# Neighbourhood attention on one core: two heads' scores in the two row halves of the array, operands loaded one pair ahead

## The chip, the core and the metric

The kernel runs on one core of a Trainium2 chip. The core has TensorE (PE, with its weight loads listed apart as PEld), VectorE (DVE), ScalarE (ACT), GpSimd (POOL) and SyncE (SP, which here only issues DMAs); each takes its own instructions in order and waits on semaphores for the others. The metric is the device time of one execution in microseconds (us); lower is better.

## The reference

A diffusion backbone of two layers works on 2048 latent tokens (a grid of 32 rows and 64 columns) of width 1024 and on 256 context tokens. The first ("even") layer has dense attention and a gated linear scan. The second ("odd") layer, which the change is about, is neighbourhood attention with 16 heads of 64: each token looks at a window of 8 x 16 grid neighbours, with a learned bias, and at all 256 context tokens, and one softmax goes over both.

```python
s_lat = jnp.einsum('bqhd,brkhd->bhqrk', qr, kb, preferred_element_type=jnp.float32) * scale
s_lat = s_lat + bias.astype(jnp.float32)[None]
s_lat = jnp.where(col_mask[None, None, :, None, :], s_lat, -jnp.inf).reshape(bsz, h, GRID_W, kr * GRID_W)
s_ctx = jnp.einsum('bqhd,bchd->bhqc', qr, k_ctx, preferred_element_type=jnp.float32) * scale
p = jax.nn.softmax(jnp.concatenate([s_lat, s_ctx], axis=-1), axis=-1).astype(v.dtype)
o = jnp.einsum('bhqk,bkhd->bqhd', p[..., :kr * GRID_W], vb.reshape(bsz, kr * GRID_W, h, d))
return o + jnp.einsum('bhqc,bchd->bqhd', p[..., kr * GRID_W:], v_ctx)
...
y = jnp.dot(o.reshape(h.shape[0], h.shape[1], C_WIDTH) * jax.nn.silu(z_x), w_out)
```

## The kernel before

The stages run one after the other, each with its own pools of tiles: the even layer up to about 1885 us, the odd layer's queries and keys (`odd_qk`) to about 2540, its values and gates (`odd_vz`) to 2970, the attention (`odd_attention`) to about 3368, and the output projection, woven with its end, to 3532. Products that need more than one pass are split in a high and a low part, so that a score is q·k = kh·qh + kl·qh + kh·ql.

`odd_vz` weaves two streams: gemms for values and gates (lines 131 to 133), and, for every head and query, a maximum of its scores (matmuls 1696 and 1703, DVE 1709 with the bias table `mtab`). To that table POOL adds a row mask and a column mask (lines 1681 and 1682). The maxima M go to memory with a minus sign, and later enter the scores as one more row, so that the exponentials cannot overflow.

`odd_attention` works on eight pairs of heads, j = 0 to 7. A pair has 20 steps in a fixed order: c0, c1, l0 to l3, c2, l4 to l7, c3, l8 to l15. Context step c*n* takes the 512 queries of block *n* against the 256 context keys (two key tiles, u = 0 and 1); local step l*n* takes the 128 keys of tile *n* against the rectangle of queries that can see them (264 to 480 wide in PE's scores).

- **Scores** (lines 1792 to 1794): for each head and key tile two matmuls into a bank `st` of 512 (four banks in turn): K's high and low halves stacked on 128 rows against the high part of Q, which stands there twice; and 65 rows, K's high part and a row of ones against Q's low part and the row M.
- **Bias and exponential**: in a local step DVE adds the bias table to each head's bank (line 1954, in 1 to 4 rectangles a head), into a tile `opt` (11 buffers) that both heads share; ACT (line 108, the helper `act`) takes the exponential. A context step has no bias, and ACT reads the bank directly, 512 at a time.
- **Tails**: a step's P·V is put off on a list `pend`. When six steps stand there, four are issued (`flush(4)`): matmuls on column halves of the array, one head in each, lines 1805 (context) and 1827 (local), into tiles `o`. The sums of P for the denominators are kept in `oacc`, by POOL (1815 and 1833) and DVE (1817).
- **Denominators**: two flushes after a block of 512 queries is complete, `finish_block` (lines 1001 to 1008) sums `oacc` over the keys on PE, again in column halves, and divides: ACT takes Ln and Exp of the sums, and DVE has three operations. POOL stores the result.
- **Loads** (line 113, all on SP in program order): keys of the local steps come in chunks of 512 (`kt`), one chunk ahead; queries, tables and values of the next pair during the pair. POOL adds the mask to both heads' tables (line 1790).

The order on each engine is the order of the program, but for places where an instruction is put behind another by hand (`issue_after`). Tiles come in turn out of their buffers, and an instruction waits until the last readers of that buffer are done.

## Time and profile before

| | us |
|---|---|
| three executions | 3533.73, 3535.8, 3543.46 |
| median | 3535.8 |
| span of the profiled execution (its own time is not listed apart) | 3532.0 |
| PE busy | 3447.5 (98%) |
| DVE busy | 2431.0 (69%) |
| ACT busy | 1450.9 (41%) |
| POOL busy | 1246.5 (35%) |

The span is the stretch between the first and the last instruction of one execution; the three times contain a little more than that. PE's ends are modelled, so it is safer to read the start of one matmul to the start of the next than the length of one. A row of a group or of the timeline reads: line, engine, operation, output tile <- input tiles, shape; "64*128" is a row half of the array (64 rows), "128*64" a column half; "x4" is four such instructions in a row. What stands behind "<-" in brackets is the instruction or the DMA that ended the idle time.

Four groups of the attention that tell what its parts cost (count, total us, mean ns, idle time before them):

```profile
L1805 PE MATMUL o<-opt,ov 128*64 128x512 f32 x256 | 62.8, 606 | 0.0
L1954 DVE TENSOR_TENSOR opt<-st,tab 128x248 f32<-128x248 f32 x64 | 25.9, 405 | 23.7 <-ACT rl L108 23.7
L108 ACT ACTIVATE opt<-st 128x512 f32<-128x512 f32 x128 | 68.6, 603 | 33.9 <-PE st L1794 32.8 <-ACT opt L108 0.9
L1833 POOL TENSOR_TENSOR oacc<-oacc,opt 128x744 f32<-128x744 f32 x32 | 52.8, 1649 | 0.6
```

### The profile page before, as it was taken

What the parts mean: (1) busy time and instruction counts of PE and PEld (TensorE: products, weight loads), DVE (VectorE), ACT (ScalarE), POOL (GpSimd) and SP (SyncE); (2) the same over time, 40 slices, a digit from 0 to 9 for tenths busy, and PEclk for the clock granted to TensorE, in tenths of its full rate; (3) what the DMA queues carried; (4) which work ended last, traced back from release to release, by engine and by line L of the source; (5) the groups of instructions that cost most, each with busy time, mean ns of one, the idle gap of its engine ahead of it and who ended that gap; (6) DMA issues with size and microseconds to landing.
All of it is one profiled execution on the core that took longest, in us unless ns stands there. A gap on an engine that the chain in (4) does not pass through costs nothing.

```text
span 3532.0 us, 54046 instructions
## 1 busy us (share of the span) xinstructions
PE 3447.5 (98%) x19460; PEld 2667.4 (76%) x19460; DVE 2431.0 (69%) x4798; ACT 1450.9 (41%) x2647; POOL 1246.5 (35%) x1400
## 2 busy tenths in 40 slices
PE   8999999999999999999999999999999999999999
PEld 6888987888896666665557878888788887555577
DVE  4677756888886777768876655444478884666775
ACT  4545552111113454546664345445322223555532
POOL 1343431111111333422211134334344443888842
PEclk9999999999999999999999999999999999999999
DMA  7555555233325242334525665455844547888684
GB/s 255 149 157 159 150 143 152 94 110 92 90 78 169 63 134 81 104 109 138 174 87 140 129 191 144 137 157 144 259 153 161 166 141 208 224 214 210 195 235 75
DMA packets 379838, 527.28 MB, mean 149 GB/s; under 512 B 34746, under 2 KB 254346, under 8 KB 373124
## 3 DMA queue, kind: packets, MB, share of 16 engines
q1 hardware_dynamic: 326692, 405.85, 39.8%
q0 software_dynamic: 29856, 82.14, 9.3%
q10 hardware_dynamic: 23024, 35.85, 2.9%
q8 instruction: 154, 2.52, 0.3%
q14 instruction: 112, 0.92, 0.1%
HBM read 344.92 MB, written 196.60 MB: 153 GB/s over the span
## 4 chain that ended last, share of the span: by engine, by line
PE 82%; DMA 6%; DVE 5%; ACT 2%; POOL 2%; issue 2%; SPq 0%; DVEq 0%; ACTq 0%; POOLq 0%
PE st L1175 10%; PE gm L133 10%; PE gm L131 10%; PE gm L132 10%; PE av L1085 7%; PE mx L705 4%; PE st L1793 2%; PE o L1827 2%; PE pu L1364 2%; PE o L1364 2%; PE st L1794 2%; PE pj L1364 1%; PE o L1805 1%; PE st L1364 1%; PE mx L1703 1%
## 5 line engine op out<-in xcount | busy, mean ns | idle before, releaser
L706 DVE TENSOR_REDUCE mm<-mx 128x1 f32<-128x512 f32 (+1 forms) x656 | 389.1, 627 | 83.6 <-PE mx L705 76.6
L108 ACT ACTIVATE apt<-st 128x1024 f32<-128x1024 f32 (+1 forms) x296 | 300.2, 1015 | 304.7 <-PE st L1175 285.5
L1182 DVE TENSOR_TENSOR acc<-acc,apt 128x1024 f32<-128x1024 f32 x256 | 341.0, 1332 | 83.0 <-ACT apt L108 64.2
L1175 PE MATMUL st<-aq,akh 64*128 64x512 f32 x1728 | 312.1, 408 | 1.2 <-ACT apt L108 0.9
L1085 PE MATMUL av<-apt,av 128*64 128x512 f32 x1152 | 267.5, 602 | 0.0
L1954 DVE TENSOR_TENSOR opt<-st,tab 128x64 f32<-128x64 f32 (+10 forms) x576 | 144.6, 315 | 146.9 <-PE st L1794 101.3
L705 PE MATMUL mx<-mk,mq 96*128 96x512 f32 (+1 forms) x656 | 236.0, 373 | 4.2 <-DMA mq<-QC 3.6
L1833 POOL TENSOR_TENSOR oacc<-oacc,opt 128x576 f32<-128x576 f32 (+5 forms) x192 | 223.5, 1186 | 40.5 <-ACT rl L108 15.0
L1175 PE MATMUL st<-aq,akl 64*128 64x512 f32 (+1 forms) x1152 | 230.6, 390 | 0.0
L108 ACT ACTIVATE u<-gm 128x352 f32<-128x352 f32 (+1 forms) x140 | 68.6, 497 | 373.7 <-PE gm L133 205.9
L1175 PEld LDWEIGHTS st<-aq,akh 64*128 64x128 f32 x1728 | 152.8, 185 | 82.8 <-ACT apt L108 29.1
L1709 DVE CUSTOM_DVE_ANT_1 mx<-mx,mtab 128x217 f32<-128x217 f32 (+14 forms) x576 | 182.2, 340 | 34.7 <-PE mx L1703 25.7
L1085 PEld LDWEIGHTS av<-apt,av 128*64 128x64 f32 x1152 | 76.7, 137 | 136.5 <-issue 135.5
L108 ACT ACTIVATE opt<-opt 128x930 f32<-128x930 f32 (+8 forms) x130 | 104.5, 805 | 105.9 <-DVE opt L1954 102.3
L705 PEld LDWEIGHTS mx<-mk,mq 96*128 96x128 f32 x656 | 121.7, 189 | 16.5 <-issue 4.0
L1175 PEld LDWEIGHTS st<-aq,akl 64*128 64x128 f32 (+1 forms) x1152 | 112.2, 184 | 22.9
L1698 DVE TENSOR_REDUCE mm<-mx 128x2 f32<-128x512 f32 x128 | 88.3, 690 | 43.1 <-PE mx L1696 41.7
L220 POOL TENSOR_TENSOR oss<-oss,mhalf 128x8 f32<-128x8 f32 x68 | 113.4, 1667 | 5.0
L131 PE MATMUL gm<-w1h,hhi 128*128 128x512 f32 x280 | 111.6, 399 | 0.0
L133 PE MATMUL gm<-w1h,hlo 128*128 128x512 f32 x280 | 110.3, 394 | 0.0
L1793 PE MATMUL st<-q,kt 128*128 128x480 f32 (+5 forms) x256 | 99.3, 390 | 11.0 <-DVE opt L1954 6.4
L132 PE MATMUL gm<-w1l,hhi 128*128 128x512 f32 x280 | 109.6, 392 | 0.0
(699 smaller groups left out, 9747.3 us busy)
## 6 DMA issues: line engine op xcount, KB each, us to landing
q<-Q SPq DMA_DIRECT2D x48, 512.0 KB
H<-x ACTq DMA_DIRECT2D x32, 512.0 KB
adaw<-ada_w SPq DMA_DIRECT2D x64, 256.0 KB
wraw<-w_od SPq DMA_DIRECT2D x64, 256.0 KB
K1t<-okt POOLq DMA_DIRECT2D x32, 512.0 KB, 9.7
kt<-K1t SPq DMA_DIRECT2D x32, 512.0 KB
x<-H SPq DMA_DIRECT2D x31, 512.0 KB
mtab<-rpb_q SPq DMA_DIRECT2D x16, 899.0 KB
```

Of the source, the lines that this page charges most:

```text
L108: return self.nc.scalar.activation(out, in_, func, **kw)
L131: self.nc.tensor.matmul(out, lh(k), rh(k), start=start and j == 0, stop=False)
L132: self.nc.tensor.matmul(out, lh(k), rl(k), start=False, stop=False)
L133: yield self.nc.tensor.matmul(out, ll(k), rh(k), start=False, stop=stop and j == n - 1)
L705: mm = nc.tensor.matmul(ps[:, :w], q[:A_QK, (t % 6) * P : (t % 6) * P + P], k[:A_QK, k0 : k0 + w], start=True, stop=True)
L706: nc.vector.tensor_reduce(out=m[:, t, n : n + 1], in_=ps[:, :w], axis=AX.X, op=ALU.max)
L1085: mm = nc.tensor.matmul(O[j, nb][i * 64 : i * 64 + 64, :w], V[j, kt // TT][:, kt % TT, i * 64 : i * 64 + 64], pts[:, i, :w], start=n == 0, ...
L1175: mm = nc.tensor.matmul(ps[:, o // 64, :w], k[o : o + r, kb, kq], Q[o : o + r, qb, :w], start=m == 0, stop=m == 4)
L1182: added = nc.vector.tensor_tensor(out=acc[:, :, :w], in0=a[:, :, :w], in1=pts[:, :, :w], op=ALU.add)
L1364: self.mm = self.nc.tensor.matmul(ps, x[:, k, :], y, start=start and k == 0 and n == 0, stop=k == self.H4 - 1 and n == 2, skip_group_check ...
L1709: nc.vector.tensor_tensor_reduce(out=s, in0=s, in1=tb[:, ri : ri + rn, ci : ci + cn], scale=1.0, scalar=-3e38, op0=ALU.add, op1=ALU.max, a ...
L1833: self.psum = nc.gpsimd.tensor_tensor(out=a, in0=a, in1=pts[:, :, a0 - r0 : a1 - r0, :], op=ALU.add)
```

## The change

**Scores.** Each head gets a row half of the array (64 rows). A score has four terms, kh·qh, kl·qh, kh·ql and ones·M, and for each term the two heads' matmuls stand next to each other. M is a tile of zeros in which only rows 0 and 64 hold the two heads' maxima, against a tile of ones. Both heads of a step (in a context step, of one key tile) write one tile `st` of two banks, of which there are two in place of four single banks. One DVE addition adds the bias for both heads; one exponential takes 1024 in a context step.

**Denominators.** `finish_blocks` treats two blocks at once: the sums of blocks 0 and 1, and those of 2 and 3, take one of the two `st` tiles; ACT copies them out, and takes Ln and Exp of 1024. `pend` holds five steps and gives two at a time (`flush(2)`).

**Loads.** Queries and keys of a pair are tiles of both heads (high and low part, without copies), in two sets of pools `oaA` and `oaB`, and the next pair's are loaded at steps 3 to 6. The stored keys `K1t` have another layout, so that `odd_qk` stores them with two DMAs instead of four. The pools stand on the left side of the memory.

**Masks.** The tables come with -1e30 filled in where a key is out of the window, so POOL adds no masks, in `odd_vz` and in the attention, and `maskq` and `maskk` are not loaded.

```diff
-            bank = lambda: self.tl(pp, [P, 512], "st", bufs=4)
+            both = lambda: self.tl(pp, [P, 2, 512], "st", bufs=2)
...
-            def scores(ps, k1, k2, q1, q2):
-                nc.tensor.matmul(ps, k1, q1, start=True, stop=False)
-                return nc.tensor.matmul(ps, k2, q2, start=False, stop=True)
+            def scores(ps, ks, qs, j):
+                terms = [(K[j][0], Q[j][0]), (K[j][1], Q[j][0]), (K[j][0], Q[j][1]), (None, M[j % 2])]
+                for n, (k, q) in enumerate(terms):
+                    for i in range(2):
+                        s = slice(i * 64, i * 64 + 64)
+                        mm = nc.tensor.matmul(ps(i), ones[s] if k is None else k[s, ks], qs(q[s]), start=n == 0, stop=n == 3)
+                return mm
...
+            def finish_blocks(bbs, j, O, acc):
+                n = len(bbs)
+                den = both()
+                for b, bb in enumerate(bbs):
+                    for i, a in enumerate(sums(acc, bb)):
+                        mm = nc.tensor.matmul(den[i * 64 : i * 64 + 64, b, :], self.mtwos[:], a, start=True, stop=True)
+                dc, rc, ln = exps(), exps(), self.tl(lp, [P, 2, 512], "rl", bufs=1)
+                self.act(dc[:, :n], den[:, :n])
+                self.act(ln[:, :n], dc[:, :n], AF.Ln, scale=-1.0)
+                self.act(rc[:, :n], ln[:, :n], AF.Exp, scale=-1.0)
+                nc.vector.tensor_tensor(out=ln[:, :n], in0=dc[:, :n], in1=rc[:, :n], op=ALU.mult)
+                for b, bb in enumerate(bbs):
+                    o = O.pop(bb)[:].rearrange("p r c -> p (r c)")
+                    nc.vector.scalar_tensor_tensor(out=o, in0=ln[:, b], scalar=2.0, in1=o, op0=ALU.add, op1=ALU.mult)
+                    nc.vector.tensor_tensor(out=rc[:, b], in0=o, in1=rc[:, b], op=ALU.mult)
...
-                                bias = nc.vector.tensor_tensor(out=pt[:, d[0], d[1]], in0=ps[:, d[0], d[1]],
-                                                               in1=tabs[j][i][:, ri : ri + rn, ci : ci + cn], op=ALU.add)
+                                bias = nc.vector.tensor_tensor(out=pt[:, :, ro : ro + rn, co : co + cn],
+                                                               in0=ps[:, :, ro : ro + rn, d + co : d + co + cn],
+                                                               in1=tabs[j][:, :, ri : ri + rn, ci : ci + cn], op=ALU.add)
...
-                    if len(pend) == 6:
+                    if len(pend) == 5:
                         with self.tc.issue_after(mm.ins):
-                            flush(4)
+                            mm = flush(2)
```

The first place is on PE, in pair 3 around the first denominators that pair 2 leaves behind (`mtwos` is a tile of constants). Before, the order there is: the end of context step c1 (`kc`), the tails of four local steps, one block's denominators, then local scores:

```order
L1793 MATMUL st_30008<-q_5211_29706,kc_5235_29807 128x512
L1794 MATMUL st_30008<-q_5212_29707,kc_4848_28046 128x512
L1827 MATMUL o_29748<-opt_29877,ov_29238 64x3x24 x2
L1827 MATMUL o_29845<-opt_29877,ov_29238 64x8x24 x2
...
L1001 MATMUL st_30032<-oacc_5179_29576,mtwos_63 64x512 x2
L1793 MATMUL st_30047<-q_5185_29595,kt_5246_29874 128x288
L1794 MATMUL st_30047<-q_5186_29596,kt_4850_28048 128x288
L1793 MATMUL st_30054<-q_5211_29706,kt_5246_29874 128x288
L1794 MATMUL st_30054<-q_5212_29707,kt_4850_28048 128x288
```

In the changed kernel the tails of two local steps and the denominators of two blocks follow context step c0, and both key tiles of c1 and local step l0 come behind them (`om` is the tile of maxima):

```order
L1787 MATMUL st_30357<-om_4850_27978,ones_27976 128x512 x2
L1817 MATMUL o_30143<-opt_30259,ov_29567 64x3x24 x2
L1817 MATMUL o_30240<-opt_30259,ov_29567 64x8x24 x2
L1817 MATMUL o_30143<-opt_30290,ov_29567 64x3x31 x2
L1817 MATMUL o_30240<-opt_30290,ov_29567 64x8x31 x2
L1838 MATMUL st_30378<-oacc_5135_29953,mtwos_63 64x512 x4
L1787 MATMUL st_30395<-qh_29965,kh_29984 128x512 x2
...
L1787 MATMUL st_30406<-qh_29965,kh_29984 128x512 x2
...
L1787 MATMUL st_30417<-qh_29965,kh_29984 128x288 x2
```

The run of column halves moved one step up and is shorter by two tails; three score tiles in a row (30395, 30406, 30417) now share two buffers with the denominators' tile (30378).

The second place is ACT around the same denominators. Before, the exponentials of both context steps are done when Ln (`rl`) and Exp (`rc`) of one block come, and local exponentials follow:

```order
L108 ACTIVATE opt_29995<-st_30004 128x512
L108 ACTIVATE opt_29995<-st_30008 128x512
L108 ACTIVATE rl_30035<-st_30032 128x512
L108 ACTIVATE rc_30036<-rl_30035 128x512
L108 ACTIVATE opt_30046<-opt_30046 128x2x288
```

After it, with the copy of the denominators, Ln and Exp of 1024 ahead of the two exponentials of c1:

```order
L108 ACTIVATE opt_30355<-st_30346 128x1024
L108 ACTIVATE opt_30366<-st_30357 128x1024
L108 ACTIVATE opt_30383<-st_30378 128x1024
L108 ACTIVATE rl_30385<-opt_30383 128x1024
L108 ACTIVATE opt_30384<-rl_30385 128x1024
L108 ACTIVATE opt_30404<-st_30395 128x1024
L108 ACTIVATE opt_30415<-st_30406 128x1024
L108 ACTIVATE opt_30418<-opt_30418 128x2x288
```

The exponential of c1's first tile (30395) moved behind three operations on the denominators.

The third place is the first loads of the attention on SP, before:

```order
L113 DMA q_4852_28054<-Q 64x2048 x2
L113 DMA q_4853_28055<-Q 64x2048
L113 DMA q_4853_28055<-M 1x2048
L113 DMA kt_4854_28060<-K1t 128x2x512
L113 DMA kt_4850_28048<-K1t 64x2x512
L113 DMA ov_28063<-V 128x16x128
L113 DMA tab_4856_28065<-rpb_k 128x1034
L113 DMA tab_4857_28066<-rpb_k 128x1034
L113 DMA ov_28069<-maskk 128x1034
L113 DMA kc_4859_28073<-K1t 128x2x256
L113 DMA kc_4848_28046<-K1t 64x2x256
L113 DMA q_4860_28076<-Q 64x2048 x2
```

and after:

```order
L113 DMA kh_27982<-K1t 128x256
L113 DMA kl_27983<-K1t 128x256
L113 DMA qh_27980<-Q 128x1024
L113 DMA ql_27981<-Q 128x1024
L113 DMA om_4848_27974<-M 1x2048 x2
L113 DMA kh_27982<-K1t 128x512
L113 DMA kl_27983<-K1t 128x512
L113 DMA tab_27992<-rpb_k 128x2x1034
L113 DMA qh_27980<-Q 128x1024
L113 DMA ql_27981<-Q 128x1024
L113 DMA ov_27996<-V1c 128x2x128
L113 DMA ov_27996<-V 128x16x128
```

The context keys and the first half of both query parts moved to the front; the values' load moved from the seventh place to behind all queries.

305 lines of the change are left out of this document (132 added, 173 removed).

## The prediction

> **What bounds the kernel now.** I read the page's busy shares first (TensorE is busy for 98% of the span), then a table of windows over the stages that the change touches, because an average over the program says nothing about one stage. In each row: the window, its length, then busy time of PE, PEld, DVE, ACT and POOL, the granted clock, the DMA share and GB/s.
>
> ```profile
> 2540.00:2945.00 405.00, 402.60 (x1994) 338.72 (x1995) 316.85 (x1353) 105.17 (x177) 177.45 (x149) 1.00 0.50 159
> 2972.94:2986.60 13.66, 13.40 (x38) 9.62 (x38) 5.68 (x26) 6.68 (x11) 2.55 (x2) 0.50 0.96 274
> 3108.02:3153.48 45.46, 44.29 (x306) 27.22 (x305) 29.54 (x89) 25.36 (x41) 38.89 (x35) 1.00 0.87 222
> ```
>
> The first row is the stage of the gemms and row maxima, where the masks go from POOL: PE has 402.60 of 405 us, so less work on POOL is worth nothing there. The third is one head pair of the attention (from its first context score to the next pair's): 45.46 us, of which PE fills 44.29, POOL 38.89, DVE 29.54, ACT 25.36. So PE sets the pair, and only what it executes, or waits for inside a pair, counts. The second row is the start of the attention: 13.66 us at half clock, so 6.8 us lost. Why it starts cold is in PE's timeline (start, length, instruction, idle time before it):
>
> ```profile
> 2969.51 0.39 PE L133 MATMUL gm<-w1h,hlo 128*128 128x512 f32 x1
> 2972.62 1.33 PE L1793 MATMUL st<-q,kc 128*128 128x512 f32 x3 [2.72 <-DMA q<-Q]
> ```
>
> PE idles 2.72 us for the first queries. Over the whole attention, PE's list of waits (total, times, longest) names two more kinds:
>
> ```profile
> PE st L1793 <- DVE opt L1954: 6.8, 19, 1.7
> PE st L1794 <- DMA kt<-K1t: 1.7, 4, 0.7
> PE st L1793 <- DMA kt<-K1t: 1.6, 2, 1.1
> ```
>
> **1. The scores themselves: 0.** A step had four full matmuls (two heads, two terms); it gets eight in row halves, which are four slots if both halves run at once. Full slots, and row-half pairs of the even layer's attention (each x2 is a pair, the x4 two):
>
> ```profile
> 3109.68 0.39 PE L1793 MATMUL st<-q,kc 128*128 128x512 f32 x1
> 3109.91 0.40 PE L1794 MATMUL st<-q,kc 65*128 65x512 f32 x1
> 1304.57 0.40 PE L1175 MATMUL st<-aq,akh 64*128 64x512 f32 x2
> 1304.81 0.39 PE L1175 MATMUL st<-aq,akl 33*128 33x512 f32 x2
> 1305.04 0.62 PE L1175 MATMUL st<-aq,akh 64*128 64x512 f32 x4
> ```
>
> Start to start is 0.23 us for one full matmul and 0.24 and 0.23 for a pair. Same slots, same widths: nothing won or lost. P·V and denominators keep their matmuls too.
>
> **2. Switches between scores and column halves: +0.6 us a pair.**
>
> ```profile
> 3111.84 0.39 PE L1794 MATMUL st<-q,kc 65*128 65x512 f32 x1
> 3112.16 2.28 PE L1827 MATMUL o<-opt,ov 128*64 128x72 f32 x32
> 3244.59 1.02 PE L1001 MATMUL st<-oacc,mtwos 128*64 128x512 f32 x4
> 3245.54 0.43 PE L1793 MATMUL st<-q,kt 128*128 128x352 f32 x1
> 3245.81 0.33 PE L1794 MATMUL st<-q,kt 65*128 65x352 f32 x1
> ```
>
> The last score to P·V takes 0.32 us in place of 0.23; two denominator slots take 0.95 in place of the 0.86 that P·V slots of that width have; and the first score behind takes 0.27 for a slot of some 0.17 (352 wide). So 0.2 us a round trip. PE's order holds 7 column runs in a pair now and 10 after (two tails at a time instead of four): +0.6 us.
>
> The Trainium skill, TensorEngine Tiling (Array Packing), Key Properties, says that changing the tiling mode, and not just the tile, drains TensorE: a rule against this change, and the trace agrees, with 0.09 us at each of these seams. It gives no price, so the sum goes by the rows.
>
> **3. PE's waits inside a pair: +0.5 us.** Widths at the slot rates above give 38.4 us of array work a pair, before and after. 45.46 less 38.4 less 7 × 0.2 leaves 5.7 us of waits now (where a matmul starts late, the list above counts only what its modelled predecessor leaves idle). Those go with the four banks that were handed round singly; in their place come two double tiles. I walked the new order on PE, ACT and DVE for one pair with these durations (group rows: count, busy, mean ns; timeline rows of ACT):
>
> ```profile
> L1954 DVE TENSOR_TENSOR opt<-st,tab 128x465 f32<-128x465 f32 x64 | 38.1, 634 | 30.4 <-POOL oacc L1833 19.8 <-PE st L1794 10.7
> L1954 DVE TENSOR_TENSOR opt<-st,tab 128x240 f32<-128x240 f32 x64 | 25.5, 398 | 4.7 <-PE st L1794 4.6
> 1299.21 1.02 ACT L108 ACTIVATE apt<-st 128x1024 f32<-128x1024 f32 x1
> 1300.14 0.59 ACT L108 ACTIVATE gqT<-gl 128x512 f32<-128x512 f32 x1
> ```
>
> A double ACT operation lasts 1.02 us and blocks ACT for 0.93. A double bias addition is not in the trace: the two DVE rows give (634 − 398)/225 = 1.05 ns an element over some 146 ns, so 930 elements are about 1.12 us (bounds: 0.63, one of now, and 2 × 0.634 = 1.27). The worst place is the denominator run ahead of context chunk 1. On ACT stand, in order, the copy of the denominators, Ln, Exp, and only then the exponentials of the two new score tiles. From the end of the run: copy done at 0.25 + 1.02 = 1.3, the exponential behind Ln and Exp starts at 0.25 + 3 × 0.93 = 3.0 and ends at 4.1. PE does c1u0 (four slots, 0.93), waits 0.3 for the copy's tile, does c1u1, and stands at 7 × 0.33 = 2.3 before l0, which needs the tile of c1u0: **a wait of about 1.9 us**. Behind it queue all later matmuls. The second denominator run costs 0.7 the same way, double bias additions with two tiles cost 0.2 to 0.5 at five more places (1.7), and at each of the ten returns to scores some 0.15 is left of the release of a tile that the column run did not cover (1.5). Sum: 1.9 + 0.3 + 0.7 + 1.7 + 1.5 = 6.1, say 6.2 us. Bounds: 3.5 us, if tiles come free as early as the four banks do, and 8.5, if DVE's five operations of the denominators also stand ahead of a bias addition each time.
>
> So a pair costs +1.1 us; pairs 1 to 7 have the denominators in them: **+8**.
>
> **4. The clock after that wait: +4.** Half clock comes in steps of 3.41 us, after windows like these:
>
> ```profile
> 3321.10:3324.52 3.42, 1.67 (x8) 0.68 (x6) 3.42 (x6) 2.60 (x5) 2.37 (x2) 1.00 0.72 222
> 3324.52:3327.93 3.41, 3.41 (x9) 2.96 (x10) 3.41 (x9) 2.34 (x5) 3.41 (x4) 0.50 0.73 183
> 3426.92:3430.33 3.41, 1.75 (x8) 1.44 (x9) 3.41 (x5) 0.63 (x1) 1.62 (x2) 1.00 0.56 156
> 3430.33:3433.74 3.41, 1.25 (x6) 0.71 (x5) 0.53 (x1) 0.60 (x1) 2.77 (x2) 1.00 1.11 198
> ```
>
> With PE busy 1.67 us of 3.42 the next window is at 0.50; with 1.75 of 3.41 it stays at 1.00. So about 1.7 us of idle time in one window is the point. Mine of 1.9, with 0.3 ahead, is just over it, and fits whole in a window about half the time: 7 × 1/2 × 1.7 us = 6 if it is as long as walked, 0 if it is 0.3 shorter; I take 4.
>
> The Trainium skill, TensorE: Matmul & The Clock Gate, Part 1, says the clock halves after an idle window of some 3.4 us, so a wait of 1.9 us would do nothing; by it the sum would be 4 us lower. The trace disagrees: half a window of idle time was enough at 3321.
>
> **5. The start: −9.5.** Loads on SP now, the last matmul of the gemm that the first new load waits for, and POOL's memsets and a store of values:
>
> ```profile
> 2936.65 1.73 SPq L113 DMA_DIRECT2D q<-Q  x3
> 2951.22 9.73 SPq L113 DMA_DIRECT2D kc<-K1t  x2
> 2961.01 1.92 SPq L113 DMA_DIRECT2D q<-Q  x3
> 2946.66 0.39 PE L133 MATMUL gm<-w3h,hlo 128*128 128x512 f32 x1
> 2945.72 1.84 POOL L1759 MEMSET kt<- 1x1024 f32 x2
> 2962.99 0.57 POOL L1614 DMA_DIRECT2D V1c<-ovz  x1 [8.46 <-ACT ovz L108]
> ```
>
> Six whole query parts (twice the high one) of 512 KB, tables, a mask and values precede what the first score needs. After, the first score needs the context keys (0.25 MB) and half of the queries (1 MB), first in SP's order; they wait for the gemm with w3 (2946.66), and at the 274 GB/s of the window at 2972.94 1.25 MB take 5 us. So they land near 2955, ahead of the gemms' end at 2969.7: 2.7 us of waiting and 6.8 of half clock go. POOL clears a row tile of 2048 first, which by the row (two of 1024 in 1.84) ends near 2950. What is late next: the first values, whose load stands behind the store of 2962.99, with the other key chunks and pair 1's loads queued behind it on SP; the first P·V needs them some 7 us after 2970, so they still have 12 us. Bounds: 0 (rival c) and 9.5.
>
> **6. Key chunks: −5.** They were loaded just ahead; a pair ahead, the waits of 1.7 + 1.6 us go, and with them one half-clock window behind two of them (−1.7):
>
> ```profile
> 3239.00:3242.40 3.40, 3.40 (x23) 2.85 (x25) 2.19 (x12) 1.28 (x2) 3.40 (x3) 0.53 0.50 157
> ```
>
> High parts are no longer loaded twice, so the DMA share of 0.87 falls as well.
>
> **7. POOL's masks, half the DVE instructions, two stores for four of keys: 0.** PE covers them (402.60 of 405). Within a pair, the masks are two additions of 2.4 us on POOL:
>
> ```profile
> L1790 POOL TENSOR_TENSOR tab<-tab,maskk 128x1034 f32<-128x1034 f32 x14 | 33.3, 2398 | 0.0
> ```
>
> POOL falls from 38.9 to about 34 us of 46, DVE from 29.5 to 25, ACT grows by the two copies (+1.9): none is the bound over a pair. The output projection gets other buffers but the same order: 0, ±4.
>
> **Sum.** +8 + 4 − 9.5 − 5 = −2.5. The profiled span is 3532.0 and the runs are 3533.73, 3535.8 and 3543.46, so it stands for an execution at the lower end, about 1.7 us longer than its span; the difference is applied to the median: 3535.8 − 2.5 = 3533.
>
> **Rivals.** (a) *The waits are hidden.* Two double tiles let PE run ahead as well as four banks did, and the wait behind the denominators stays under the clock's point: part 3 takes its lower bound, 3.5 us in place of 6.2, and part 4 nothing. 7 × −2.7 − 4 = −23: 3510. For it speaks that the even layer's attention, with the same double tiles and 1.02 us exponentials, hardly waits for them; against it, that no Ln and Exp stand between its scores:
>
> ```profile
> L1175 PE MATMUL st<-aq,akh 64*128 64x512 f32 x1728 | 312.1, 408 | 1.2 <-ACT apt L108 0.9
> ```
>
> (b) *Slower: every denominator run drops the clock for two windows.* Place: l0 of pairs 1 to 7; price: 6.8 us at half clock, 3.4 each, 24 in place of 4; it decides from 1.7 us of idle time in a window. 3553. For it: at 2972.94 half clock lasted four windows; against it: at 3239.00 one window was enough to come back. (c) *The start is not won*, because the first operands wait for memory of the last gemms: +9.5: 3543. Against it: SP's order names a gemm well ahead of the last. (d) *Row halves run one after the other*: 96 more slots a pair, 18 us × 8: 3680; the even layer's rows speak against it.
>
> **Chances.** The sum 0.39, (a) 0.32, (b) 0.20, (c) 0.08, (d) 0.01. A measurement of this kernel can tell about 0.3%, 10.6 us, from no change: the limits are 3525 and 3546. The sum's own range is 3523 to 3544 (parts 3, 4 and 7). Faster: (a) and a corner of the sum, 0.34. Slower: (b), (d), a third of (c) and a corner of the sum, 0.26. Same: 0.40. The range reaches past (b) and, for the part of it that falls short of its bound, nearly through (a): 3509 to 3556.
>
> **What would show it.** Step 1: pairs of L1787 at 0.23 us start to start. 2: ten runs of column halves in a pair, 0.2 us each. 3: PE waiting near 1.9 us for ACT at l0, behind the denominators' run; pair periods near 46.5. 4: windows at 0.50 behind them. 5: the first L1787 within 0.3 us of the last gemm, at full clock. 6: no wait of L1787 for K1t. It would be wrong if POOL, which frees the buffers of the exponentials, held ACT, or if pair 1's loads, 6.6 MB behind one another, came late.

## The result, and the profile after

The changed kernel takes 3557.6 us (median of four executions, 3553.0 to 3563.8), the kernel before 3539.6 beside it (3533.7 to 3543.5): a ratio of 1.0056, with a 95% interval of 1.0038 to 1.0074. It is slower by 0.4 to 0.7%. The profiled spans are 3551.2 and 3532.0 us, 19.2 apart.

To see where the 19.2 us arise, the span is cut at four places that both traces have: the first score, pair 1's first context score, pair 7's, and the last score. The rows are windows, with the columns of the prediction's first fence. Of the kernel before:

```profile
2972.62:3017.67 45.05, 43.57 (x260) 29.50 (x261) 21.51 (x69) 21.11 (x33) 30.13 (x25) 0.85 0.90 221
3017.67:3293.28 275.61, 266.52 (x1825) 164.27 (x1825) 177.66 (x529) 152.12 (x241) 232.32 (x205) 0.99 0.88 221
3293.28:3348.41 55.13, 49.09 (x306) 29.89 (x305) 49.35 (x104) 34.10 (x57) 42.77 (x35) 0.94 0.53 167
3348.41:3532.00 183.59, 172.05 (x740) 135.63 (x740) 120.56 (x159) 50.58 (x71) 70.35 (x52) 0.96 0.67 159
```

And of the changed kernel, with its row for pair 3 alone as the last:

```profile
2962.75:3001.26 38.51, 37.48 (x353) 24.88 (x354) 17.84 (x34) 19.79 (x23) 29.84 (x26) 1.00 0.68 246
3001.26:3290.92 289.66, 266.37 (x2405) 167.18 (x2402) 150.63 (x288) 158.42 (x181) 201.97 (x168) 0.99 0.44 164
3290.92:3354.16 63.24, 51.78 (x409) 31.74 (x406) 47.79 (x67) 36.04 (x50) 39.22 (x29) 0.89 0.33 104
3354.16:3551.20 197.04, 174.29 (x744) 136.41 (x740) 126.75 (x151) 52.06 (x71) 70.33 (x51) 0.95 0.67 150
3097.46:3145.93 48.47, 43.98 (x404) 27.47 (x402) 25.91 (x48) 26.32 (x31) 34.23 (x29) 1.00 0.43 161
```

| stretch | before | after | difference | forecast |
|---|---|---|---|---|
| up to the last gemm ahead of the attention | 2969.5 | 2961.7 | −7.8 | 0 (part 7) |
| last gemm to first score | 3.1 | 1.1 | −2.0 | −2.7 (part 5) |
| pair 0 | 45.1 | 38.5 | −6.5 | −6.8 (part 5) |
| pairs 1 to 6 | 275.6 | 289.7 | +14.1 | +5.0 (parts 2, 3, 4, 6) |
| pair 7, to the last score | 55.1 | 63.2 | +8.1 | +1.7 (parts 2, 3, 4) |
| behind the last score | 183.6 | 197.0 | +13.4 | 0 (part 7) |

In pairs 1 to 6 PE is as busy as before (266.4 and 266.5 us); the 14 us are waiting. DVE and POOL have less to do (150.6 for 177.7, 202.0 for 232.3), the DMA share is halved, and none of that helps. PE's waits of the attention (total, times, longest) now name ACT first:

```profile
PE st L1787 <- ACT opt L108: 24.7, 32, 2.3
PE st L1787 <- DVE opt L1946: 10.5, 16, 2.4
```

The place is the one that the prediction walked through. PE's timeline of pair 3 at the two-block denominators (L1838), then ACT's and DVE's of the same time:

```profile
3101.04 1.88 PE L1838 MATMUL st<-oacc,mtwos 128*64 128x512 f32 x8
3102.86 0.50 PE L1787 MATMUL st<-qh,kh 64*128 64x512 f32 x2
...
3107.26 0.40 PE L1787 MATMUL st<-qh,kh 64*128 64x288 f32 x2 [1.97 <-ACT opt L108]
...
3111.08 0.45 PE L1787 MATMUL st<-qh,kh 64*128 64x384 f32 x2 [0.93 <-DVE opt L1946]
```

```profile
3103.03 1.03 ACT L108 ACTIVATE opt<-st 128x1024 f32<-128x1024 f32 x1 [1.75 <-PE st L1838]
3104.09 1.06 ACT L108 ACTIVATE rl<-opt 128x1024 f32<-128x1024 f32 x1
3105.24 1.06 ACT L108 ACTIVATE opt<-rl 128x1024 f32<-128x1024 f32 x1
3106.21 1.92 ACT L108 ACTIVATE opt<-st 128x1024 f32<-128x1024 f32 x2
```

```profile
3106.33 1.23 DVE L1843 TENSOR_TENSOR rl<-opt,opt 128x1024 f32<-128x1024 f32 x1 [7.64 <-ACT opt L108]
3107.59 1.29 DVE L1846 SCALAR_TENSOR_TENSOR o<-rl,o 128x512 f32<-128x512 f32 x2
...
3109.40 0.61 DVE L1946 TENSOR_TENSOR opt<-st,tab 128x64 f32<-128x64 f32 x3
```

Copy, Ln and Exp stand ahead of the two exponentials of c1, which start at 3106.21 and hold both score tiles; so PE waits 1.97 us for l0's (forecast: about 1.9). But it doesn't end there. Two steps later PE waits again, 0.93 us, for DVE: l0's scores were there at 3108, and their bias addition starts at 3109.40, behind four of the division's five operations.

Behind the last score PE's list of waits shows that DVE became late (before, no wait there is longer than 2.7 us):

```profile
PE st L1364 <- DVE rc L1315: 7.9, 1, 7.9
...
PE st L131 <- DVE rc L1315: 3.5, 1, 3.5
```

DVE must sum and convert weights there (L1327, L1299). The first row of each pair is SP's loads of those weights, the second DVE's first sum; before, then after:

```profile
3359.53 9.27 SPq L113 DMA_DIRECT2D opt<-w_out  x8
3363.31 0.69 DVE L1327 TENSOR_TENSOR opt<-opt 128x512 f32<-128x512 f32 x1 [9.70 <-DMA opt<-w_out]
```

```profile
3366.45 16.78 SPq L113 DMA_DIRECT2D opt<-w_out  x8
3381.67 1.83 DVE L1327 TENSOR_TENSOR opt<-opt 128x512 f32<-128x512 f32 x1
```

Counted from the last score, the sums begin 14.9 us later before and 27.5 after.

### The profile page after: what moved, and what is told of

Same layout as the page of the kernel before. It is cut to its first block, busy times and chain, and to the rows that moved or that the text cites. A ratio compares the mean times of both kernels' runs of the same rounds, so it can differ in the third digit from the quotient of the medians.

```text
span 3551.2 us, 54744 instructions
## 1 busy us (share of the span) xinstructions
PE 3438.4 (97%) x20228; PEld 2663.4 (75%) x20228; DVE 2407.6 (68%) x4479; ACT 1461.6 (41%) x2570; POOL 1079.6 (30%) x1296
## 4 chain that ended last, share of the span: by engine, by line
PE 81%; DVE 6%; DMA 5%; ACT 4%; POOL 2%; issue 2%; SPq 0%; ACTq 0%; DVEq 0%; POOLq 0%
PE st L1175 10%; PE gm L133 10%; PE gm L131 10%; PE gm L132 10%; PE av L1085 7%; PE mx L705 4%; PE st L1787 3%; PE o L1817 2%; PE pu L1364 2%; ACT opt L108 1%; PE o L1364 1%; PE o L1799 1%; PE pj L1364 1%; PE mx L1697 1%; PE st L1364 1%
## 5 line engine op out<-in xcount | busy, mean ns | idle before, releaser
L1823 POOL TENSOR_TENSOR oacc<-oacc,opt 128x528 f32<-128x528 f32 (+4 forms) x192 | 229.4, 1218 | 63.7 <-ACT opt L108 38.6
L1703 DVE CUSTOM_DVE_ANT_1 mx<-mx,mtab 128x105 f32<-128x105 f32 (+14 forms) x576 | 183.1, 340 | 46.2 <-PE mx L1697 34.7
L1946 DVE TENSOR_TENSOR opt<-st,tab 128x496 f32<-128x496 f32 (+16 forms) x288 | 122.9, 485 | 129.8 <-PE st L1787 129.8
L1787 PE MATMUL st<-qh,kh 64*128 64x512 f32 (+6 forms) x384 | 84.0, 431 | 36.5 <-ACT opt L108 24.7
L1552 DVE TENSOR_TENSOR onat<-gm,oss 128x512 f32<-128x512 f32 x68 | 46.9, 690 | 95.7 <-POOL oss L220 95.7
L131 PE MATMUL gm<-w0h,hhi 128*128 128x512 f32 x272 | 109.6, 403 | 0.0
```

Of the source, the lines that this page charges most:

```text
L131: self.nc.tensor.matmul(out, lh(k), rh(k), start=start and j == 0, stop=False)
L1703: nc.vector.tensor_tensor_reduce(out=s, in0=s, in1=tb[:, ri : ri + rn, ci : ci + cn], scale=1.0, scalar=-3e38, op0=ALU.add, op1=ALU.max, a ...
L1787: mm = nc.tensor.matmul(ps(i), ones[s] if k is None else k[s, ks], qs(q[s]), start=n == 0, stop=n == 3)
L1823: nc.gpsimd.tensor_tensor(out=a, in0=a, in1=pts[:, :, a0 - r0 : a1 - r0, :], op=ALU.add)
```

## The experiments

**Theory A**: the pairs lose to the division of the denominators, because with two tiles for scores neither ACT nor DVE has room for it between two steps. **Theory B**: the rest is lost behind the last score, by buffers that the changed kernel shares there (exponentials, score tiles). Rivals: the seams of the row halves, the double bias additions, or a wait that only changes its name. All results stand in one table; "pair" is the usual period of pairs 1 to 6, "attention" goes from the first score to the end of the span, "end" from pair 7's first score; "one" is a single execution. The first score itself lies between 2960 and 2971 us in the kernels made from the changed one (2969 to 2979 in those made from before), which no edit in the attention touches; so the stretches say more than the spans.

| | pair | attention | end | median us | ratio (95%) |
|---|---|---|---|---|---|
| before | 45.4 | 559.4 | 238.7 | 3539.6 | |
| changed | 48.4 | 588.5 | 260.3 | 3557.6 | 1.0056 (1.0038 to 1.0074) |
| e1_nodiv | 44.4 | 550.9 | 245.6 | 3519.5, one | |
| e11_before_nodiv | 44.1 | 552.7 | 235.4 | 3533.3, one | |
| e5_noact | 47.8 | 580.3 | 255.0 | 3542.5, one | |
| e6_nodve | 48.4 / 47.0 | 577.2 | 252.4 | 3544.6, one | |
| e2_defer | 48.7 / 50.3 | 593.0 | 259.1 | 3562.6 | 1.0083 (1.0067 to 1.0098) |
| e8_single | 50.6 | 605.7 | 262.6 | 3571.0 | 1.0091 (1.0074 to 1.0108) |
| e7_banks | 50.2 | 587.4 | 243.7 | 3559.3 | 1.0058 (1.0039 to 1.0077) |
| e12_flush4 | 50.6 | 605.8 | 259.7 | 3572.2, one | |
| e3_tail_old | 48.5 | 595.2 | 267.0 | 3558.6 | 1.0075 (1.0060 to 1.0090) |
| e9_tail_copy | 48.5 | 594.0 | 264.8 | 3560.2 | 1.0063 (1.0048 to 1.0079) |
| e13_obanks | 48.6 | 589.9 | 260.6 | 3553.5 | 1.0053 (1.0039 to 1.0067) |
| e16_tail_both | 48.5 | 593.5 | 264.3 | 3563.0 | 1.0073 (1.0058 to 1.0088) |
| e14_obanks_defer1 | 47.5 | 575.5 | 251.9 | 3547.0 | 1.0036 (1.0023 to 1.0049) |
| e17_tail_both_defer1 | 47.5 | 581.6 | 254.6 | 3545.9 | 1.0028 (1.0015 to 1.0042) |
| e4_masks | 44.9 | 562.8 | 240.8 | 3533.3 | 1.0001 (0.9991 to 1.0010) |
| e10_start | 44.9 to 45.5 | 557.6 | 236.8 | 3532.5 | 0.9992 (0.9982 to 1.0001) |
| e15_masks_v10 | 44.9 | 554.2 | 242.7 | 3524.4 | 0.9970 (0.9959 to 0.9981) |

### The division taken out of both kernels

e1 is the changed kernel with the sums and their copy, but without Ln, Exp and DVE's five operations; e11 takes the same out of the kernel before (it copies the sums too, so that there is something to store).

```diff
-                self.act(ln[:, :n], dc[:, :n], AF.Ln, scale=-1.0)
-                self.act(rc[:, :n], ln[:, :n], AF.Exp, scale=-1.0)
-                nc.vector.tensor_tensor(out=ln[:, :n], in0=dc[:, :n], in1=rc[:, :n], op=ALU.mult)
...
```

> The changed kernel without the division of the odd attention (no Ln, no Exp, no DVE operations of the denominators; the sums are still made, copied and stored, in all eight pairs), so its output is not the attention's. Theory A (the denominators' chain on ACT and DVE, ahead of the next scores' exponentials and bias additions, makes the waits of a pair): PE's waits of 2.2 us at l0 and about 1.2 at l2 go in pairs 1 to 7, periods fall from 48.3 to about 44.5, no half clock behind them; span 3551 - 27 - 5 and some of the end: 3510 to 3520. Rival B (two double score tiles instead of four banks lose at every step): only about 1 us a pair goes, periods 47, span near 3544.

> The kernel before without the division of the odd attention (no Ln, no Exp, no DVE operations of the denominators; the sums are made, copied to where the reciprocal stood, and stored), so its output is not the attention's. In the changed kernel the division cost 4.1 us of a pair. If single blocks and four banks hide it: periods fall from 45.5 by 1 us at most, to 44.5 to 45.5. If the division costs as much before: periods near 41.5.

One pair of e1, and one of e11:

```profile
3094.21:3138.60 44.39, 43.34 (x405) 27.63 (x403) 18.73 (x38) 22.70 (x27) 33.75 (x29) 1.00 0.49 176
3115.58:3159.66 44.08, 43.66 (x306) 27.27 (x305) 22.17 (x77) 23.21 (x36) 38.53 (x35) 1.00 0.88 228
```

Without the division the two kernels' pairs differ by 0.3 us. With it, the changed kernel pays 48.5 − 44.4 = 4.1 us a pair, the one before 45.5 − 44.1 = 1.4. So the division carries the loss within the pairs; seams, double additions, filled tables and the new loads together come to about 0.3. That is a net figure: e11 still has POOL's masks, without which the kernel before gains 0.6 us a pair (e4, below), so the seams and double additions may cost up to 0.9, and no run separates them. In pair 7 and the stretch behind it, the division goes with 14.7 us in the changed kernel (260.3 to 245.6) and 3.3 in the one before (238.7 to 235.4): 11.4 of the 21.6 us lost there, and 10.2 stay.

### Only ACT's part, only DVE's part

e5 leaves out Ln and Exp and keeps DVE's operations; e6 leaves out those and keeps Ln and Exp.

> The changed kernel without Ln and Exp of the odd attention's denominators (the copy and the five DVE operations stay, working on the copy), so its output is not the attention's. Division as a whole cost 4.1 us of a 48.3 us pair. If ACT's queue makes the waits: l0 no longer waits 2.2 us, DVE's operations start 2.1 us earlier and are out of the way of l0's bias addition, so nearly all goes: periods 44.5 to 45.5. If DVE's five operations ahead of the bias additions make them: periods 46.5 to 47.5.

> The changed kernel without the five DVE operations of the odd attention's denominators (copy, Ln and Exp stay; the reciprocal is stored in place of the quotient), so its output is not the attention's. If ACT's queue makes the waits: l0 still waits about 2 us, periods 46.5 to 47.5. If DVE's operations make them: periods 44.5 to 45.5.

Taken alone, ACT's part gives 0.6 us of the 4.1 and DVE's at most 1.5; together they give all. e6's two periods differ by the clock: it is 0.96 in each pair of 48.4 us and 1.00 in each of 47.0. e5's period and e6's longer one lie above what either forecast gave. Either chain is long enough to hold PE by itself, so a list of waits that names ACT doesn't say that ACT alone is to blame.

### The division put off

e2 issues Ln and Exp behind the next context exponential and DVE's operations behind the next bias addition (pairs 0 to 6).

```diff
+                            if u == 0 and put_off and len(put_off[0]) == 2:
+                                with self.tc.issue_after(ex.ins):
+                                    put_off[0].pop(0)()
...
+                        if put_off and len(put_off[0]) == 1:
+                            with self.tc.issue_after(bias.ins):
+                                put_off.pop(0)[0]()
```

> The changed kernel with Ln and Exp put behind the next context exponential and the DVE part of the denominators behind the next local step's bias addition (pairs 0 to 6). Theory A: the 2.2 us at l0 go, about 1 us comes back at l1, which then waits for the second tile: -2 to -3 us a pair, periods 45.5 to 46.5, half clock in pairs gone; span 3551 - 7 x 2.2 - 5 = 3531, with the end as it is. Rival B: the wait only moves, span 3546 to 3551.

PE's waits of the attention in e2, and the second denominators of a pair:

```profile
PE st L1787 <- DVE opt L1958: 14.9, 24, 2.0
PE st L1838 <- DVE opt L1958: 12.9, 8, 1.7
...
3120.04 3.45 PE L1838 MATMUL st<-oacc,mtwos 128*64 128x512 f32 x8 [1.68 <-DVE opt L1958]
```

The wait at l0 is gone (in the pairs at full clock c0 to c2 takes 19.4 us in place of 21.0). But a bias addition that stands behind the division on DVE now comes later, the denominators' run of blocks 2 and 3 waits 1.7 us for its tile, and in two of pairs 1 to 6 the clock falls there (3.45 us for a run that took 1.88), which makes 50.3 of 48.7. The forecast of theory A missed: the wait moved to the next place.

### More tiles, shorter holds

e7 gives the changed kernel four single banks, a bias addition and an exponential for each head, the denominators by single block as before, and the old lists (six steps, four at a time). e12 changes only the lists; e8 only the denominators, one block at a time with a copy.

```diff
-            both = lambda: self.tl(pp, [P, 2, 512], "st", bufs=2)
...
+            bank = lambda: self.tl(pp, [P, 512], "st", bufs=4)[:]
...
-                    if len(pend) == 5:
+                    if len(pend) == 6:
...
-                            mm = flush(2)
+                            mm = flush(4)
```

> The changed kernel with one part undone: four single score banks, a bias addition for each head, context exponentials of 512, denominators one block at a time with Ln from the bank and buffers of their own, six pending steps and flushes of four, all as before; row halves, loads a pair ahead and filled tables stay. Theory A (double tiles together with the double denominators make the loss): periods 44.5 to 45, the start and the first pair keep their 16 us, no long wait for DVE in the projection: 3506 to 3515, faster than before by 0.5% or more. Rival (the row halves or the pair-ahead loads themselves cost the time): periods 47 or more, 3535 or more.

> The changed kernel with six pending steps and flushes of four, as before, so with 5 to 7 runs of column halves in a pair in place of 10. If the seams (0.15 us at each end of a run) cost the time: -0.75 to -1.5 us, periods 46.7 to 47.5. If two steps in flight bound a stretch of four score steps (as in the run with single banks, whose stretches lost 1.7 to 2.9 us each): periods 49 to 51.

> The changed kernel with only the merging of the denominators undone: one block of 512 at a time, at the places of before, copied out of the score tile, reciprocal and copy not in the exponentials' buffers; two double score tiles, double bias additions and flushes of two stay. If the double burst (3 us on ACT, 3.7 on DVE) is what the two tiles cannot cover: periods 45.5 to 46.5, projection's waits for DVE gone, 3520 to 3530. If two tiles are the cause by themselves: periods 47.5 to 49, as four blocks now take a tile four times a pair, 3545 to 3560.

Here theory A was wrong as first put: with four banks a pair takes 50.2 us, and the forecast was 44.5 to 45. But these are not the same waits. In one pair of e7 PE is busy for 48.9 of the 50.2 us, in the changed kernel for 44.0 of 48.5, both at full clock. A context step in e7's timeline:

```profile
3086.34 0.47 PE L1780 MATMUL st<-qh,kh 64*128 64x512 f32 x1
3086.65 0.39 PE L1780 MATMUL st<-qh,kl 64*128 64x512 f32 x1
3086.83 0.47 PE L1780 MATMUL st<-qh,kh 64*128 64x512 f32 x1
3086.88 0.39 PE L1780 MATMUL st<-ql,kh 64*128 64x512 f32 x1
```

The second head's first matmul (3086.83) starts 0.49 us behind the first head's (3086.34), and each head then goes through its terms at its own time. Of a pair's 192 score matmuls some 100 start within 0.06 us of another; in the changed kernel and in e12 all 192 do. So with single banks PE idles less, but only about half of the matmuls start beside one of the other row half. A likely reason is that the two heads' banks come free one after the other, a double tile for both at once; no run shows this by itself.

e12, with the double tiles and nothing but the lists changed, has nearly the same period, 50.6, with PE busy for only 43.8. Its waits for the bias additions are 26.5 us in total, 10.5 in the changed kernel: with longer score stretches between the tails, each stretch runs into the limit of two steps. e7 has these lists too, and four banks with the changed kernel's own lists weren't tried. In the kernel before, one head's bank was full, and DVE at work on it, while PE was still at the other head's. e8 takes a tile four times a pair instead of twice. Its one pair of 1 to 6 at full clock takes 48.9 us, the others, at 0.93 to 0.97, take 50.3 to 52.0; so most of what it loses more than the changed kernel is the clock.

### Behind the last score

e3 treats pair 7's denominators block by block, with Ln read from the bank and buffers of their own, so that the exponentials' tiles come free for the weights; e9 does the same with a copy first; e13 puts the projection's gemms of tiles 1 to 3 on the four banks of P·V; e16 is e3 and e13 together.

```diff
+                if j == 7:
+                    for bb in bbs:
+                        mm = finish_one(bb, j, O, acc)
+                    return mm
...
+            obank = lambda: self.tl(pp, [P, 8, 64], "o", bufs=4)[:].rearrange("p r c -> p (r c)")
...
-                steps = self.project_steps(hi, lo, None, gate, wout, bank, y, out[t * P : t * P + P, :])
+                steps = self.project_steps(hi, lo, None, gate, wout, obank, y, out[t * P : t * P + P, :])
```

> The changed kernel with the last pair's denominators done as before: one block at a time, Ln from the bank, the reciprocal in a buffer of its own and not in one of the eleven buffers of the exponentials. Theory T (buffers taken by the last denominators hold up the weight loads of the projection and, behind them, DVE's weight sums): the loads end near 3370 instead of 3383, PE's waits of 3.5 and 7.9 us for DVE in the projection go, and the half clock at 3420: 3551 - 11 - 3 = 3537. Rival U (DVE is late because the last pair as a whole ends late and its order is fixed): the two waits stay, 3548 to 3551.

> The changed kernel with the last pair's denominators one block at a time, the copy and the reciprocal in small buffers of their own (not in the exponentials' eleven), and, other than in the run before of that kind, the score tile given back by the copy. Theory T (the last denominators' buffers and their double DVE operations hold up the loads and DVE's work on the projection's weights, and so PE): the projection's gemms lose 15 us more than their array time, as before, in place of 30; 3551 - 15 = 3536. Rival U (the late end of pair 7 itself makes DVE late): they still lose 25 or more, 3546 to 3551.

> The changed kernel, but the projection's first three row tiles (t = 1 to 3) take single banks in turn out of the four of the finished outputs, in place of the halves of the two double score tiles. Theory W (a half is given back only with its tile, so PE's gemms wait for DVE results that stand behind the weight sums): the waits of 3.5 and 7.9 us for DVE go, the last stretch loses 15 to 18 us over its array time as before in place of 30: 3551 - 12 to 15 = 3536 to 3539. Rival T (DVE and ACT are late with the weights themselves): the waits move to the weights, 3547 to 3555.

> The changed kernel with both edits of the tail: pair 7's denominators per block, with Ln read from the bank and buffers of their own (as in e3), and the output projection's gemms of tiles 1 to 3 on the four single banks of P.V (as in e13). Theory B2 (two causes, each enough by itself: the tiles of the exponentials that keep the weights out, and the score tile that waits for DVE): PE's wait of 13.4 us for L1839 goes, and no wait of over 3 us for L1299 takes its place, since DVE's first weight sum comes 12.7 us after the last score instead of 26.4; the projection ends 183 to 188 us after the last score instead of 196 to 197, and the span is 3544 to 3549. Rival W (DVE's time for weight sums and products is the bound, whatever PE waits for by name): the wait moves to L1299 or L1327, the projection ends 193 or more after the last score, span 3553 or more. The pairs 1 to 6 stay at 48.2 in both.

PE's longest wait behind the last score in e3, and then in e16; in e9 it is 13.6 us for ACT with a split of the weights (L1364), in e13 8.1 us in three waits for DVE's conversions (L1299):

```profile
PE st L131 <- DVE rl L1839: 13.4, 1, 13.4
```

```profile
PE o L131 <- DVE rc L1842: 16.9, 1, 16.9
```

Theory B fell in all four: the wait took another name each time. e16's DVE shows why. Its timeline (from the division of one block to that of the next):

```profile
3378.41 0.69 DVE L1839 TENSOR_TENSOR rl<-st,rc 128x512 f32<-128x512 f32 x1
...
3380.38 1.77 DVE L1327 TENSOR_TENSOR opt<-opt 128x512 f32<-128x512 f32 x1 [0.34 <-DMA opt<-w_out]
...
3396.44 0.68 DVE L1327 TENSOR_TENSOR opt<-opt,opt 128x512 f32<-128x512 f32 x1
3397.04 0.68 DVE L1839 TENSOR_TENSOR rl<-st,rc 128x512 f32<-128x512 f32 x1
```

Between two blocks' divisions stand some 16 us of work almost without a gap, most of it weight sums and conversions. The tile that the division reads or holds (a score tile in e3, a bank of P·V in e16) comes free only then. That points to the place of the division in DVE's order, whichever tile is held.

e14 is e13 with the division of blocks 0 and 1 alone put off; e17 is e16 with that, and with two buffers for the logarithms of pair 7, so that the last division stands further ahead on DVE (3.3 us behind the one before it, 15.0 in e16).

> As the run with single banks in the projection, and Ln and Exp of blocks 0 and 1 alone put behind the first context exponential of c1, their DVE operations behind l0's bias addition (blocks 2 and 3 stay where they were). If each of the two denominator runs is a wait of its own: c0 to c2 falls from 21.0 to 19.4 as in the run that put off both, and the rest of the pair stays at 27.2: periods 46.6, 3536 - 11 = 3525. If what is put off comes back in the rest of the pair: periods 48 or more, 3535 to 3540.

> e16 with a second buffer for the logarithms of pair 7 (the other pairs take a tile of the exponentials for them), and Ln, Exp and the DVE operations of blocks 0 and 1 put off as in e14. Theory B2: pairs near 47.5 as in e14 and the tail of e16, so a span of 3536 to 3543, level with the kernel before (ratio 1.000 to 1.003). Rival W: 3547 or more.

e17 cuts the one wait of 16.9 us to 5.5 and 4.3, and the stretch behind the last score to 188.3 us; e14 brings the pairs to 47.5 (c0 to c2 19.4 us for 21.0, c2 to c3 12.2 for 11.3). The pairs lie between e14's two forecasts, 46.6 and 48. By their medians both kernels are better than the changed one, though the intervals of their ratios overlap with its own, and both are still slower than the one before. e17's span of 3544.1 lies 1 us above its forecast: in pairs 1 and 6 the clock is 0.97, and they take 49.2.

e7 goes furthest: its stretch behind the last score is 183.3 us, as long as before (183.6), and PE's longest wait there is 3.3 us for DVE's conversions. It keeps the row halves, the loads a pair ahead and the filled tables, so these don't cost the time behind the last score; what does is among the things that e7 undoes (double tiles, denominators of two blocks, shared buffers, lists). The lists alone don't (e12: 196.5).

### The other parts, on the kernel before

e4 is the kernel before with the filled tables and without POOL's masks. e10 adds an order of the first loads like the changed kernel's, context keys and queries first. e15 is e4 with the next pair's values loaded at l10 instead of l6.

```diff
-                            with self.tc.issue_after(self.psum.ins):
-                                mask(tabs[j + 1])
...
-                        elif (kind, n) == ("l", 6):
+                        elif (kind, n) == ("l", 10):
                             V[j + 1] = values(j + 1)
```

> The kernel before with only the masks filled into the tables (no POOL additions, no mask loads). As predicted, PE covers all of it: 3532, same as before within 3 us. Rival: POOL's mask additions held exponentials' buffers and the mask's load the first queries: the first score comes 2 us earlier without half clock and the pair period falls by 0.5 us: 3520 to 3525.

> The kernel before with filled tables, and with the attention's first loads in another order: context keys, both heads' queries, the first key chunk, tables, values, the second chunk. If the order of the first loads made PE wait and the clock fall: the first score follows the last gemm within 0.5 us at full clock, 9 us less than the kernel with filled tables: 3523 to 3526, 0.2 to 0.3% faster than before. Rival (the 13 MB of doubled operands cannot come sooner): the wait moves to the key chunks or the values, 3530 to 3533.

> The kernel before with filled tables, and the next pair's values loaded at l10 in place of l6. In the run with filled tables alone the load of the values held SP for 9.5 us ahead of a key chunk, for which PE then waited 4.5 and 0.5 us, while the pairs without such a wait took 44.9 in place of 45.5 us. If that is where the gain of the filled tables went: no wait over 1 us for key chunks, periods 44.9 throughout: 3532 - 6 - 3 = 3523 to 3527, faster than before by 0.3%. Rival: the next pair's keys and queries come late in turn, 3530 to 3534.

In e4 a pair is 0.6 us shorter (44.9), but two pairs wait for keys. PE's wait, and what stood ahead of the keys on SP:

```profile
PE st L1789 <- DMA kt<-K1t: 6.1, 2, 4.5
```

```profile
2988.57 9.50 SPq L113 DMA_DIRECT2D ov<-V1c  x1
2998.17 1.26 SPq L113 DMA_DIRECT2D kt<-K1t  x2
```

SP stands 9.5 us at the context values (the trace doesn't tell for what), and the keys queue behind it. Reordering only the first loads moves that wait (e10: pair 0 takes 50.2 us). Asking for the values later removes it: in e15 the keys' waits are down to 0.9 us, pairs 1 to 6 take 44.9 each, and the kernel is faster than the one before by 0.3% (0.2 to 0.4%), as forecast. Of the kernels that compute the whole attention it is the only one that is clearly faster than both.

## Why the prediction was wrong

- **Start (part 5, −9.5)**: right. The first score follows the last gemm after 1.08 us in place of 3.11, at full clock, and pair 0 is 6.5 us shorter: −8.5 in all. The sign it named, a first score within 0.3 us of the last gemm, didn't come. That the order of the loads does it isn't shown either: e4, with the old order and only the masks gone, has its first score 1.09 us after the last gemm, and full clock in the 12 us behind it.
- **Scores and seams (parts 1 and 2)**: right for the scores: row-half pairs start 0.23 us apart. Without the division the kernels' pairs differ by 0.3 us, where 0.6 was put for the seams. As the filled tables may hide part of the cost, the seams are not shown by themselves.
- **Key chunks (part 6, −5)**: right; no wait for K1t is left. Its price isn't shown by itself; e15 shows that the kernel before, with the tables filled, needs only a later load of values to be rid of nearly all of these waits.
- **The clock (part 4, +4)**: the number of falls was right, their price was less here. Behind the denominators the clock fell in pairs 1, 6 and 7, three of the seven. Pairs 5 and 6, the second with such a window:

```profile
3193.87:3242.35 48.48, 44.01 (x405) 27.48 (x402) 25.97 (x48) 26.33 (x31) 34.24 (x29) 1.00 0.43 161
3242.35:3290.92 48.57, 45.20 (x405) 28.68 (x402) 24.75 (x48) 26.43 (x31) 33.35 (x29) 0.96 0.47 172
```

  PE is busy for 1.2 us more in the second, and the pair is longer by 0.1: the slow matmuls lie where PE would have waited for ACT or DVE. Pairs 2 and 4, at full clock, take 47.6 and 47.9, so the price is 0.1 to 0.9 us, not 1.7. That holds for this kernel alone: in e2 and e17 a pair with such a window is 1.7 us longer than one without, in e6 1.4 to 1.5.
- **Waits inside a pair (part 3, +0.5)**: this term was mis-sized. It measures about +2.7 (48.4 − 45.4, less the 0.3 that stay without the division), and the periods are near 48.4, not 46.5. By the prediction's own count that is 5.7 + 2.7 = 8.4 us of waits, where 6.2 was taken. The walk had the wait at l0 (1.97 for 1.9; its "7 × 0.33" stands for two times 0.93 and the 0.3 between them, which is 2.2) and stopped there: it let PE, ACT and DVE start level at the next step. In the trace DVE is still busy with the division when l0's scores arrive, and later steps wait in turn. The forecast named DVE's five operations ahead of a bias addition as the upper bound, 8.5 us, and took nearly none of it; e5, e6 and e1 show that this chain alone is enough to hold PE, so the bound was the likely case.
- **The output projection (part 7, "other buffers but the same order: 0, ±4")**: this step failed, by 13 us. The buffers are what sets when weights arrive and when a tile comes back, and DVE's place for the division of the last blocks changed with them. Of the 21.6 us lost from pair 7's start to the end, 11.4 go with the division (e1 against e11), and with the old tiles, denominators, buffers and lists the stretch behind the last score is back at 183.3 us (e7). Half clock adds to pair 7: its clock is 0.89, and was 0.94.
- **Two stores for four of keys (part 7, 0)**: missed on the other side. The last gemm ahead of the attention ends 7.8 us earlier, and 7.4 of it come in the stage of queries and keys (from the even layer's last score to the first maximum, 652.4 us for 659.8). The kernels with two stores take 651 to 657 us there, the five with four stores 660 to 663. PE's waits don't tell why: before, the first maximum waits 3.3 us for its keys (`mk`) and after 0.2, but e4 and e15, with four stores, don't have that wait, and e2, with two, has 2.9. Whether the stores or another part of the change do it wasn't tried alone.

Of the rivals, (b) gave nearly the time, 3553, but by luck and not by its mechanism: it asked for half clock in all seven pairs, and it was three. (a) and (d) are out; (c) didn't happen.

**Open**: e14's end is still 13 us, e17's 16 us and e7's 5 us longer than that of the kernel before. That the waits go when e7 undoes tiles, denominators, buffers and lists together is shown. That DVE's order around the last blocks is what makes them fits e16 and e17, but no run changes this order alone. Four single banks with the changed kernel's lists, and a pair of e7 without the division, weren't tried.

## What to carry to other kernels

Two heads side by side in the row halves cost no array time as long as both can start together; with a tile that comes free for both at once they did, with single banks they drifted apart (e7). They also finish together, so the same banks hold half as many independent steps; what else wants a tile, ACT or DVE between two steps must then fit in what one step leaves. When a kernel with a part taken out is the evidence, take the same part out of the other kernel too: 3.3 of the 14.7 us that the end gained without the division, it gained in the kernel before as well. When walking a new order, go on past the first wait until all engines are level again, and take a chain that would hold an in-order engine ahead of the next step's work as the case, not as the bound. A wait that only moves under three different edits probably belongs to an engine's order, and not to the tile that its row names.

## What the runs showed of the hardware

A DVE operation that takes 0.69 us elsewhere lasted ten times as long while POOL multiplied. Behind the changed kernel's last score, DVE's rows and POOL's:

```profile
3397.37 0.69 DVE L1299 TENSOR_TENSOR tab<-opt,ov 128x512 fp32r<-128x512 f32 x1
...
3399.17 6.84 DVE L1299 TENSOR_TENSOR ql<-opt,qh 128x512 fp32r<-128x512 f32 x1
```

```profile
3399.54 2.67 POOL L2000 TENSOR_TENSOR opt<-opt,opt 128x1024 f32<-128x1024 f32 x1
...
3402.43 5.85 POOL L2000 TENSOR_TENSOR opt<-opt,opt 128x1024 f32<-128x1024 f32 x2
```

The Trainium skill, SBUF — State Buffer, SBUF: two separate sides, says that DVE and GpSimd share one pair of ports, which an operation holds alone to its end, and that a DVE operation with two operands in that memory can lose it. The trace agrees in kind: the two stretches lie over each other. DVE's row starts 0.37 us ahead of POOL's, so the rows don't show which of the two had to wait for the other first. No run here took the products away, so it isn't shown by an experiment, and its 6 us are at most a part of the 13 behind the last score.
